# Projecting the values of the dilated heads transposed, one pair of heads at a time, and turning them on TensorE

## The chip, the cores and the metric

One core of one Trainium2 chip runs one launch of the kernel. The metric is the device time of that launch in microseconds (us), taken over several runs. A profiled execution gives the trace that the sections below read. Its engines are TensorE (PE; PEld is its weight load), VectorE (DVE), ScalarE (ACT), GpSimd (POOL) and SyncE (SP, which issues nearly all transfers; "SPq" is its queue).

## The reference, cut to what matters

One decoder layer on 512 tokens of width 1024, all in float32: a SwiGLU feed-forward, a mixer, a second SwiGLU feed-forward, each behind an RMS norm, and a final norm. The change lies in the mixer:

```
h = RMSNorm(x);  [q | k | v of 12 A heads | q | k | v of 8 B heads | gate_A | gate_B] = h @ W_in
y_A = window attention; heads 0-3 see single tokens, heads 4-7 every 4th, heads 8-11 every 16th token
      y_A of head h = merge of heads h, 4 + h, 8 + h
y_B = block attention of the 8 B heads
x = x + (sigmoid(gate_A) * (y_A @ W_up_A) + sigmoid(gate_B) * (y_B @ W_up_B)) @ W_out
```

A dilated head (4 to 11) attends within classes of tokens. The kernel works with four classes, tokens t with the same t mod 4, and needs the values of a dilated head as four tiles of 128 tokens of one class by 64 features.

## The kernel before, in words

**Numbers.** Every float32 operand of a matmul is split into a high and a low part (fp32r), and a product is three matmuls: high by high, high by low, low by high. `mac` (lines 203 to 208) issues the three. Activations are kept transposed, 8 tiles `XN[k]` of 128 features by 512 tokens, and a projection of 128 columns is 8 `mac` calls, 24 matmuls of 512 columns. The scale of the RMS norm is applied after the product: `factors` (L244) makes one row of it, `rrow`, for all tokens, and `columns` (L259) picks it as columns for token tiles.

**Weights.** One list, `stream`, holds the 512 KB weight tiles in order of use. `weights` (L193) returns the next, splits the one behind it (cast on ScalarE L189, subtraction on VectorE L190) and starts the transfer of the third behind it on the SP queue (L171).

**Mixer.** It begins inside the last tile of the first feed-forward: `FIRST` lists what is projected before the attention, `BESIDE` what is projected beside each of its 16 stages. Stages alternate: the scores of a head (`dsa_scores`, for head h the heads h, 4 + h and 8 + h), then its weighted sum. `blend` mixes the steps of a stage (main) and of its projections (side) evenly; a side step is one `mac`. The items are `qk n` (Q and K of the n-th pair of `PAIRS`: pair 0 is heads 0 and 1, pair 1 is heads 4 and 8, pair 2 is heads 5 and 9), `v c` (values of four undilated heads), `vd` (values of the dilated heads) and `g` (gates).

- `qk` : `project` and `stacked` (L459 to L485). The 128 by 512 sums of Q or K are scaled by `rrow` into a scratch tile `qkv` (L469, VectorE; dilated pairs are put in class order here), cast (L471, ScalarE), subtracted (L472, VectorE) into `qkhl` (2 buffers), and four transfers on the SP queue move the halves to Q (L483) or K (L485) tiles. The scratch tile has **one buffer, tag `ssq`**, which the row of the norm (`step`) uses before it.
- `vd` : `values_by_class` (L521). All eight heads at once. The 16 tiles of `XN` are copied on ScalarE with their tokens in class order (L534, `xc`, 3 buffers for each half). The copies are the stationary operands and 512 columns of weights move: 32 `mac` calls into **four** PSUM banks of the group `acc`, which has four and is also used by `qk`, `v` and `g`. `keep_values` then splits the sums (L517 ScalarE, L518 VectorE).

**Order.** TensorE runs in the order in which the program is written. The order on the other engines and on the SP queue is set when the kernel is built, by a planner that takes whatever is ready in its own model, earlier written first; on the chip each queue keeps that order.

```
FIRST = [("qk", 0), ("qk", 1), ("qk", 2), ("vd", 0)]
BESIDE = [ [("v", 0)], [("qk", 3)],  [("g", 0)], [("qk", 4), ("g", 1, 0)], ...
heads = [dsa(h) for h in range(4)] + [moba(h) for h in range(0, NB, 2)]
```

Of the kernel before, what the change touches and what calls it, by code (L numbers as in the profile page):

```python
# [23 lines left out]
F32 = mybir.dt.float32  # L24
# [4 lines left out]
P = 128  # L29
# [20 lines left out]
def slopes(n):  # L50
# [4 lines left out]
LAG = 2  # L55
WAIT = 5
LEAD = 9


FIRST = [("qk", 0), ("qk", 1), ("qk", 2), ("vd", 0)]  # L60
BESIDE = [
    [("v", 0)], [("qk", 3)],
    [("g", 0)], [("qk", 4), ("g", 1, 0)],
    [("qk", 5)], [("qk", 6)],
    [("g", 1, 1), ("v", 3)], [("qk", 7)],
    [("qk", 8)], [("v", 4)],
# [28 lines left out]
def decoder_layer(ctx: ExitStack, tc: tile.TileContext, xT, gains, gus, gu1, dn1, wqk, wv, wvd, wg, wup, wout, gu2, dn2, base, out):  # L95
# [35 lines left out]
    make_identity(nc, ident)  # L131


    cols_of = {}
    for name, shape in (("rcol0", [P, NT]), ("rcol1", [P, NT]), ("nv0", [P, 4, 2]), ("nv1", [P, 4, 2]), ("round", [P, 32])):
        cols_of[name] = cpool.tile(shape, F32, name=name)


    CHUNKS = [slice(c * P, min(c + 8, FT) * P) for c in range(0, FT, 8)]

    def mixer_tiles(what, n, *js):
        src = {"qk": lambda j: wqk[2 * n + j], "v": lambda j: wv[max(0, n - 2), j], "vd": lambda j: wvd[j], "g": lambda j: wg[2 * n + j]}[what]
        return [((what, n, j), src(j)) for j in js or range(4 if what == "vd" else 2)]

    def down_tiles(i, dn):
        return [((i, "d", m, c), dn[m][:, cut]) for m in range(KT) for c, cut in enumerate(CHUNKS)]
# [109 lines left out]
        newton(y, z, a, row)  # L256
        return row

    def columns(row, dilated):  # L259

        col = cols_of[f"rcol{int(dilated)}"]
        rest = tpool.tile([P, P], F32, name="rest", tag="fu")
        for t in range(NT):
            nc.vector.tensor_tensor_reduce(rest, tokens(row, t, dilated), ident, 1.0, 0.0, ALU.mult, ALU.max,
                                           accum_out=col[:, t:t + 1])
        return col

    def tokens(x, t, dilated):

        return by_class(x)[:, t] if dilated else x[:, t * P:(t + 1) * P]  # L270


    def first_tiles():
# [61 lines left out]
    def last_tile(A):  # L335

        m = KT - 1
        halves = [slice(h * HALF, (h + 1) * HALF) for h in range(2)]
        ps = [bank("all")[:, :HALF] for _ in range(2)]
        pc = [bank("all")[:, :2] for _ in range(2)]  # L340
        pr = [bank("all")[:, :HALF] for _ in range(2)]
        sq = [tpool.tile([P, HALF], F32, name=f"sql{h}", tag=("fg", "fu")[h]) for h in range(2)]
        v = [cols_of[f"nv{h}"] for h in range(2)]

        def some(h, k):
            mac(ps[h], cols(ws[k // 8], k % 8), [x[:, halves[h]] for x in A[k]], k == 0, k == FT - 1)

        def close(h):
            x = X[m][:, halves[h]]
            nc.vector.scalar_tensor_tensor(x, ps[h], 0.5, x, ALU.mult, ALU.add)  # L350
            nc.scalar.activation(sq[h], x, AF.Square)

        def sums(h, x, first):
            for t in range(2):
                nc.tensor.matmul(pc[h][:, t:t + 1], x[:, t * P:(t + 1) * P], ones[:, 0:1], start=first and t == 0,
                                 stop=not first and t == 1)

        def spread(h):
            a, y, z, col = (v[h][:, n] for n in range(4))
            nc.vector.tensor_scalar(a, pc[h], 1.0 / D, EPS, ALU.mult, ALU.add)  # L360
            newton(y, z, a, col)
            diag = tpool.tile([P, 2, P], F32, name="diag", tag=("fg", "fu")[h])
            for t in range(2):
                nc.vector.tensor_scalar(diag[:, t], ident, col[:, t:t + 1], None, ALU.mult)
            return diag

        def write(h, diag):
            nc.tensor.matmul(pr[h], ones, diag.rearrange("p t q -> p (t q)"), start=True, stop=True)
            row = tpool.tile([P, HALF], F32, name="rrow", tag=("rrow", "ssq")[h], bufs=1)
            nc.scalar.copy(row, pr[h])  # L370

            def scaled():
                for k in range(KT):
                    o = outs[h, k]
                    if k == m:
                        nc.vector.scalar_tensor_tensor(o, X[k][:, halves[h]], gain(k), pr[h], ALU.mult, ALU.mult)
                    elif k % 3 == 1 if h else k < 6:
                        nc.gpsimd.tensor_tensor(o, o, row, ALU.mult)
                    else:
                        nc.vector.tensor_tensor(o, o, pr[h], ALU.mult)  # L380
                    if k % 2:
                        nc.sync.dma_start(out[h, k // 2], pairs[h, k // 2].rearrange("p k t -> p (k t)"))
            return scaled

        def gain(k):
            return g_sb[:, 3 * KT + k:3 * KT + k + 1]

        pairs, outs = {}, {}
        for h in range(2):
            for k in range(KT):  # L390
                if k % 2 == 0:
                    pairs[h, k // 2] = xpool.tile([P, 2, HALF], F32, name=f"yo{h}_{k}", tag=f"xh{k + h}")
                outs[h, k] = pairs[h, k // 2][:, k % 2]
                if k != m:
                    nc.scalar.mul(outs[h, k], X[k][:, halves[h]], gain(k))
        ws = [weights(2, "d", m, 0)]
        for k in range(8):
            some(0, k)
            some(1, k)
        ws.append(weights(2, "d", m, 1))  # L400
        ws.append(weights(2, "d", m, 2))
        for k in range(8, FT):
            some(0, k)
        close(0)
        for h in range(2):
            sums(h, SSQ[3][:, halves[h]], True)
        for k in range(8, FT):
            some(1, k)
            if k == 11:
                sums(0, sq[0], False)  # L410
                diag = spread(0)
            if k == FT - 2:
                first = write(0, diag)
        close(1)
        sums(1, sq[1], False)
        diag = spread(1)
        first()
        warm_up(9)
        write(1, diag)()
# [18 lines left out]
    with ExitStack() as mix:  # L438
# [56 lines left out]
        def values(c):  # L495
# [11 lines left out]
                            k == 0 and t % 2 == 0, k == KT - 1 and t % 2 == 1)  # L507
                        yield
            for t in range(NT):
                keep_values(t, c, ps[t // 2][:, (t % 2) * n:(t % 2 + 1) * n], R["col"][False])  # L510

        def keep_values(t, c, pv, col):

            v = V[t, c] = mp.tile([P, 4 * P], F32R, name=f"v{t}_{c}", tag=f"v{t}_{c % 3}", bufs=1)
            heads = v.rearrange("p (h c) -> p h c", c=P)
            pv = pv.rearrange("p (h c) -> p h c", c=HD)
            nc.scalar.mul(heads[:, :, :HD], pv, col[:, t:t + 1])  # L517
            nc.vector.scalar_tensor_tensor(heads[:, :, HD:], pv, col[:, t:t + 1], f32(heads[:, :, :HD]),  # L518
                                           ALU.mult, ALU.subtract)

        def values_by_class():  # L521

            ps = [bank("acc") for _ in range(NT)]
            n = 8 * HD
            for quarter in range(4):
                w = weights("vd", 0, quarter)
                for kk in range(2):
                    k = 2 * quarter + kk  # L530
                    copies = []
                    for x, tag in zip(XN[k], ("pth", "ptl")):
                        xc = mp2.tile([P, S], F32R, name="xc", tag=tag, bufs=3)
                        nc.scalar.copy(xc.rearrange("p (r i) -> p r i", r=NT), by_class(x))  # L534
                        copies.append(xc)
                    for r in range(NT):
                        mac(ps[r], [x[:, r * P:(r + 1) * P] for x in copies], cols(w, kk, n), k == 0, k == KT - 1)
                        yield
            for r in range(NT):
                for c in (1, 2):  # L540
                    keep_values(r, c, ps[r][:, (c - 1) * 4 * HD:c * 4 * HD], R["col"][True])

        def bias(*parts):

# [93 lines left out]
        def weighted(steps, ytile, half, classes=False):  # L638
# [9 lines left out]
            for at in range(len(steps) + LAG):  # L648
# [20 lines left out]
                if at >= LAG:  # L669
                    for v, to, first, n in steps[at - LAG][1]:  # L670
                        for x in parts[at - LAG]:
                            done += 1
                            nc.tensor.matmul(to(po), V[v[0], v[1] // 4][:, v[1] % 4 * P:(v[1] % 4 + 1) * P], x[:, first:first + n],  # L673
                                             start=done == 1, stop=done == 2 * n_products)
                yield
            a, b = slice(half * HD, (half + 1) * HD), slice((1 - half) * HD, (2 - half) * HD)
# [68 lines left out]
        def part(what, n, *js):  # L745
# [3 lines left out]
            if what == "v":  # L749
                return values(n), NT * KT  # L750
            if what == "vd":
                return values_by_class(), NT * KT
            js = js or range(2)
            return (step for j in js for step in gate(n, j)), len(js) * KT


        early = []
# [2 lines left out]
                pass  # L760
            early.append(ps)
        R["row"] = factors(1, bank("out"))
        R["col"] = [columns(R["row"], dilated) for dilated in (False, True)]
        for j in range(2):
            stacked(0, j, early[j])
        for item in FIRST[1:]:
            for _ in part(*item)[0]:
                pass

        heads = [dsa(h) for h in range(4)] + [moba(h) for h in range(0, NB, 2)]  # L770
        for at, main in enumerate(x for h in heads for x in h):
            lead = LEAD * (2 if BESIDE[at][0][0] == "v" else 1)
            blend(main, [part(*item) for item in BESIDE[at]], lead if at % 2 else 0)


        YS = []
# [134 lines left out]
```

## Time and profile before

| | |
|---|---|
| median of 3 runs | 1140.09 us (1139.19 to 1141.45) |
| the profiled execution, its own time | 1141.3 us |
| its span, first to last instruction | 1139.4 us |
| mean granted clock of TensorE | 0.994 of full speed |
| busy share: PE, DVE, ACT, POOL | 98%, 52%, 38%, 2% |
| first matmul of the mixer, of the scores of head 0 | 365.8 us, 434.1 us |

A time in the text is that of the trace, in us from the start of the span. A row of a timeline gives start, duration, engine, line, operation, and in brackets how long the engine had been idle and what ended that. Matmuls overlap, so the distance between two starts is what a matmul costs, and not its duration.

### The profile page before, as it was taken

Reading aid. Unit: us, or ns where it says so; the run is one execution under the profiler, and the core shown is the slowest. Engines: PE = TensorE matmul, PEld = TensorE weight load, DVE = VectorE, ACT = ScalarE, POOL = GpSimd, SP = SyncE. Lnnn points to the kernel's source line nnn. Section 1 sums busy time; section 2 is a strip of 40 time slices with the busy share of each in tenths; the row PEclk is TensorE's granted clock in tenths of the full one; section 3 lists DMA queues with packets and bytes.
Section 4 is the critical chain, followed back from the end, with each engine's and each line's share of the span. In section 5 each row is a group of like instructions: output and inputs, shape, how many; then the busy total and the mean of one; then the engine's idle time right before and its main releaser. Section 6 shows DMA issues by size and latency. Waiting matters only on the chain.

```text
span 1139.4 us, 13537 instructions
## 1 busy us (share of the span) xinstructions
PE 1122.2 (98%) x5316; PEld 940.4 (83%) x5316; DVE 598.1 (52%) x976; ACT 429.1 (38%) x657; POOL 18.7 (2%) x34
## 2 busy tenths in 40 slices
PE   9999999999999989999999999999999999999997
PEld 7888888888888768888898888888888888888886
DVE  6744445433333637767777668654644445433323
ACT  5532233222223455444454454433333223223321
POOL 0000000000000000000000000000000000000001
PEclk9999999999999989999999999999999999999999
DMA  6222322233333382456354213332322232233321
GB/s 222 93 93 96 100 100 93 93 102 91 100 102 116 100 219 85 129 148 167 107 153 129 76 47 102 111 96 93 107 93 93 95 109 93 93 102 86 99 83 74
DMA packets 37710, 122.12 MB, mean 107 GB/s; under 512 B 4880, under 2 KB 4880, under 8 KB 37648
## 3 DMA queue, kind: packets, MB, share of 16 engines
q1 hardware_dynamic: 37072, 120.08, 34.1%
q10 hardware_dynamic: 576, 1.20, 0.3%
q8 instruction: 41, 0.67, 0.2%
q14 instruction: 21, 0.17, 0.0%
HBM read 103.44 MB, written 2.10 MB: 93 GB/s over the span
## 4 chain that ended last, share of the span: by engine, by line
PE 64%; DVE 2%; DMA 1%; ACT 1%; issue 0%; SPq 0%; DVEq 0%; ACTq 0%
PE ps_all L208 11%; PE ps_all L206 11%; PE ps_all L207 11%; PE ps_acc L206 8%; PE ps_acc L207 8%; PE ps_acc L208 8%; PE ps_out L673 2%; PE ps_att L654 1%; PE ps_att L207 1%; PE ps_att L208 1%; PE ps_att L206 1%; PE ps_att L629 1%; DMA ks<-qkhl 1%; PE ps_att L571 0%; DVE wlo L190 0%; PE ps_att L583 0%
## 5 line engine op out<-in xcount | busy, mean ns | idle before, releaser
L189 ACT CAST whi<-raw 128x1024 fp32r<-128x1024 f32 (+2 forms) x201 | 203.0, 1012 | 546.2 <-PE ps_all L207 254.9
L190 DVE TENSOR_TENSOR wlo<-raw,whi 128x1024 fp32r<-128x1024 f32 (+2 forms) x202 | 236.3, 1172 | 173.6 <-ACT whi L189 173.4
L206 PE MATMUL ps_all<-xh,whi 128*128 128x512 f32 x672 | 261.4, 389 | 0.0
L207 PE MATMUL ps_all<-xl,whi 128*128 128x512 f32 x672 | 261.4, 389 | 0.0
L208 PE MATMUL ps_all<-xh,wlo 128*128 128x512 f32 x672 | 261.4, 389 | 0.0
L207 PEld LDWEIGHTS ps_all<-xl,whi 128*128 128x128 f32 x672 | 126.1, 188 | 26.4
L208 PEld LDWEIGHTS ps_all<-xh,wlo 128*128 128x128 f32 x672 | 126.1, 188 | 26.1
L206 PEld LDWEIGHTS ps_all<-xh,whi 128*128 128x128 f32 x672 | 126.1, 188 | 26.1
L206 PE MATMUL ps_all<-ah,whi 128*128 128x512 f32 (+1 forms) x374 | 141.2, 377 | 0.0
L208 PE MATMUL ps_all<-ah,wlo 128*128 128x512 f32 (+1 forms) x374 | 140.8, 377 | 0.0
L207 PE MATMUL ps_all<-al,whi 128*128 128x512 f32 (+1 forms) x374 | 140.8, 376 | 0.0
L206 PE MATMUL ps_acc<-xh,whi 128*128 128x512 f32 x272 | 110.4, 406 | 0.0
L208 PE MATMUL ps_acc<-xh,wlo 128*128 128x512 f32 x272 | 106.4, 391 | 0.0
L207 PE MATMUL ps_acc<-xl,whi 128*128 128x512 f32 x272 | 106.3, 391 | 0.0
L297 DVE TENSOR_TENSOR fu<-ps_all,rrow 128x512 f32<-128x512 f32 x44 | 30.4, 691 | 124.1 <-PE ps_all L208 124.1
L206 PEld LDWEIGHTS ps_all<-ah,whi 128*128 128x128 f32 x374 | 70.4, 188 | 13.0
L207 PEld LDWEIGHTS ps_all<-al,whi 128*128 128x128 f32 x374 | 70.4, 188 | 13.0
L208 PEld LDWEIGHTS ps_all<-ah,wlo 128*128 128x128 f32 x374 | 70.4, 188 | 12.7
L295 DVE TENSOR_TENSOR fg<-ps_all,rrow 128x512 f32<-128x512 f32 x44 | 30.4, 691 | 79.8 <-PE ps_all L208 79.7
L208 PEld LDWEIGHTS ps_acc<-xh,wlo 128*128 128x128 f32 x272 | 51.1, 188 | 11.4
L207 PEld LDWEIGHTS ps_acc<-xl,whi 128*128 128x128 f32 x272 | 51.4, 189 | 7.2
L206 PEld LDWEIGHTS ps_acc<-xh,whi 128*128 128x128 f32 x272 | 51.2, 188 | 7.2
(168 smaller groups left out, 1256.3 us busy)
## 6 DMA issues: line engine op xcount, KB each, us to landing
raw<-in_gu_dram SPq DMA_DIRECT2D x84, 512.0 KB, 3.4
raw<-in_dn_dram SPq DMA_DIRECT2D x32, 512.0 KB, 3.5
raw<-in_wqk_dram SPq DMA_DIRECT2D x20, 512.0 KB, 3.5
ks<-qkhl SPq DMA_DIRECT2D x40, 256.0 KB, 4.9
raw<-in_wg_dram SPq DMA_DIRECT2D x16, 512.0 KB, 3.5
raw<-in_dn_dram SPq DMA_DIRECT2D x16, 384.0 KB, 3.1
qs<-qkhl SPq DMA_DIRECT2D x40, 128.0 KB, 2.5
raw<-in_wout_dram SPq DMA_DIRECT2D x8, 512.0 KB, 3.4
```

The costliest lines, as they stand in the source:

```text
L189: nc.scalar.copy(hi[:, s], raw[:, s])
L190: nc.vector.tensor_tensor(lo[:, s], raw[:, s], f32(hi[:, s]), ALU.subtract)
L206: nc.tensor.matmul(ps, wh, xh, start=first, stop=False)
L207: nc.tensor.matmul(ps, wh, xl, start=False, stop=False)
L208: nc.tensor.matmul(ps, wl, xh, start=False, stop=last)
L295: nc.vector.tensor_tensor(g, ps[0], R, ALU.mult)
L297: nc.vector.tensor_tensor(u, ps[1], R, ALU.mult)
L629: nc.tensor.matmul(ps[:, :n], Q[NA + h][:, i * P:(i + 1) * P], K[NA + h][:, part, :n], start=part == 0, stop=part == 1)
L654: nc.tensor.transpose(pt[:, n * P:(n + 1) * P], block, ident)
L673: nc.tensor.matmul(to(po), V[v[0], v[1] // 4][:, v[1] % 4 * P:(v[1] % 4 + 1) * P], x[:, first:first + n], start=done == 1, stop=done == 2 ...
```

## The change

The dilated values are projected the other way round: 128 columns of weights (one pair of heads) are stationary and the 512 tokens move, 24 matmuls into one PSUM bank, as for `qk`. VectorE scales the sums by `rrow` and puts the tokens in class order in one instruction, into the scratch tile with tag `ssq` (`vt`). Four TensorE transposes turn it into a bank of the group `att`, and a ScalarE copy and a VectorE subtraction split it. The transposes (`turned`) are issued behind the 6th step of whatever item follows. There are four such items, `vd 0` to `vd 3` (heads 4 and 5, 6 and 7, 8 and 9, 10 and 11). Two stand in `FIRST`, two move beside the scores and the weighted sum of head 1. `qk 1` becomes the last item of `FIRST`, and `qk 2` moves beside the scores of head 0. The copies `xc`, the second set of columns of the norm and the four wide banks go. The tiles of the values get other tags, and the host lays out the same weights differently.

```diff
-FIRST = [("qk", 0), ("qk", 1), ("qk", 2), ("vd", 0)]
+LATER = 5
+FIRST = [("qk", 0), ("vd", 0), ("vd", 2), ("qk", 1)]
 BESIDE = [
-    [("v", 0)], [("qk", 3)],
-    [("g", 0)], [("qk", 4), ("g", 1, 0)],
+    [("qk", 2), ("v", 0)], [("qk", 3)],
+    [("vd", 1), ("g", 0)], [("vd", 3), ("qk", 4), ("g", 1, 0)],
...
-    def columns(row, dilated):
+    def columns(row):
...
-            ps = [bank("acc") for _ in range(NT)]
-            n = 8 * HD
-            for quarter in range(4):
-                w = weights("vd", 0, quarter)
-                for kk in range(2):
-                    k = 2 * quarter + kk
-                    copies = []
-                    for x, tag in zip(XN[k], ("pth", "ptl")):
-                        xc = mp2.tile([P, S], F32R, name="xc", tag=tag, bufs=3)
-                        nc.scalar.copy(xc.rearrange("p (r i) -> p r i", r=NT), by_class(x))
-                        copies.append(xc)
-                    for r in range(NT):
-                        mac(ps[r], [x[:, r * P:(r + 1) * P] for x in copies], cols(w, kk, n), k == 0, k == KT - 1)
-                        yield
+        def values_by_class(n):
+            w = weights("vd", n, 0)
+            ps = bank("acc")
+            for k in range(KT):
+                mac(ps, cols(w, k), XN[k], k == 0, k == KT - 1)
+                yield
+            vt = tpool.tile([P, S], F32, name="qkv", tag="ssq", bufs=1)
+            nc.vector.tensor_tensor(vt.rearrange("p (r i) -> p r i", r=NT), by_class(ps), by_class(R["row"]), ALU.mult)
+            TURN.append((n, vt))
+
+        def turned():
+            n, vt = TURN.pop()
+            pt = bank("att")
             for r in range(NT):
-                for c in (1, 2):
-                    keep_values(r, c, ps[r][:, (c - 1) * 4 * HD:c * 4 * HD], R["col"][True])
+                nc.tensor.transpose(pt[:, r * P:(r + 1) * P], vt[:, r * P:(r + 1) * P], ident)
+            v = mp.tile([P, NT, 2, P], F32R, name=f"vd{n}", tag=f"vd{n}", bufs=1)
+            x = pt.rearrange("p (r h c) -> p r h c", r=NT, h=2)
+            nc.scalar.copy(v[:, :, :, :HD], x)
+            nc.vector.tensor_tensor(v[:, :, :, HD:], x, f32(v[:, :, :, :HD]), ALU.subtract)
...
+        def parts(items):
+            for item in items:
+                for at, _ in enumerate(part(*item)[0]):
+                    if at == LATER and TURN:
+                        turned()
+                    yield
+            if TURN:
+                turned()
...
-        R["col"] = [columns(R["row"], dilated) for dilated in (False, True)]
+        R["col"] = columns(R["row"])
         for j in range(2):
             stacked(0, j, early[j])
-        for item in FIRST[1:]:
-            for _ in part(*item)[0]:
-                pass
+        for _ in parts(FIRST[1:]):
+            pass
...
-            blend(main, [part(*item) for item in BESIDE[at]], lead if at % 2 else 0)
+            blend(main, [(parts(BESIDE[at]), sum(part(*item)[1] for item in BESIDE[at]))], lead if at % 2 else 0)
...
-        "wvd": _moving(v[:, 256:768], 2),
+        "wvd": _tiles(v[:, 256:768]),
```

## Rows read from the trace of the kernel before

**Rows 1.** What TensorE waited for: releaser, us in total, times, longest.

```profile
PE ps_acc L206 <- DVE qkv L469: 4.7, 2, 2.8
PE ps_att L206 <- ACT xh L222: 1.8, 1, 1.8
```

**Rows 2.** Timeline of TensorE, 365 to 382 us, the projection of pair 0.

```profile
365.83 0.39 PE L206 MATMUL ps_att<-xh,whi 128*128 128x512 f32 x1
...
370.37 0.39 PE L208 MATMUL ps_att<-xh,wlo 128*128 128x512 f32 x1
372.57 0.50 PE L206 MATMUL ps_att<-xh,whi 128*128 128x512 f32 x1 [1.82 <-ACT xh L222]
...
381.27 0.39 PE L250 MATMUL ps_out<-sl,ones_r 128*128 128x512 f32 x1
381.50 0.39 PE L206 MATMUL ps_acc<-xh,whi 128*128 128x512 f32 x1
```

**Rows 3.** Timeline of ScalarE, 366 to 373 us.

```profile
366.77 1.13 ACT L534 CAST xc<-xh 128x512 fp32r<-128x512 f32 x1
...
371.80 0.72 ACT L222 ACTIVATE xh<-x,g_sb 128x512 fp32r<-128x512 f32 x1
```

**Rows 4.** Timeline of VectorE, the end of the first feed-forward.

```profile
366.03 0.69 DVE L330 SCALAR_TENSOR_TENSOR x<-ps_all,x 128x512 f32<-128x512 f32 x1 [1.99 <-PE ps_all L208]
```

**Rows 5.** Timeline of TensorE, 403 to 433 us, all of `vd`.

```profile
403.26 0.39 PE L206 MATMUL ps_acc<-whi,xc 128*128 128x512 f32 x1
...
404.39 0.39 PE L208 MATMUL ps_acc<-whi,xc 128*128 128x512 f32 x1
...
407.57 0.47 PE L206 MATMUL ps_acc<-whi,xc 128*128 128x512 f32 x1 [2.79 <-DVE qkv L469]
...
410.39 0.76 PE L206 MATMUL ps_acc<-whi,xc 128*128 128x512 f32 x1 [1.89 <-DVE qkv L469]
...
432.90 0.36 PE L206 MATMUL ps_acc<-whi,xh 128*128 128x256 f32 x1 [0.21 <-DVE v L518]
```

**Rows 6.** Stretches: length, busy us of each engine, PEclk, DMA share, GB/s.

```profile
375.00:377.00 2.00, 2.00 (x6) 1.52 (x5) 1.83 (x2) 0.54 (x2) 0.00 (x0) 0.50 0.02 4
...
411.00:415.00 4.00, 4.00 (x11) 3.13 (x10) 0.69 (x1) 1.81 (x3) 0.00 (x0) 0.50 0.86 204
...
450.00:460.00 10.00, 10.00 (x56) 8.43 (x56) 8.41 (x22) 4.92 (x8) 0.00 (x0) 1.00 0.54 150
```

**Rows 7.** Timeline of TensorE, four transposes in a weighted sum.

```profile
453.90 0.60 PE L654 MATMUL ps_att<-ident,prow 128*128 128x128 f32 x4
454.25 0.48 PE L206 MATMUL ps_acc<-xh,whi 128*128 128x512 f32 x1
454.57 0.40 PE L207 MATMUL ps_acc<-xl,whi 128*128 128x512 f32 x1
```

**Rows 8.** Timeline of VectorE, 390 to 398 us, from `rrow` on.

```profile
390.28 0.68 DVE L241 SCALAR_TENSOR_TENSOR rrow<-step,root 128x512 f32<-128x512 f32 x1
...
391.63 0.69 DVE L469 SCALAR_TENSOR_TENSOR qkv<-ps_att,rrow 128x512 f32<-128x512 f32 x1
...
393.49 0.69 DVE L472 TENSOR_TENSOR qkhl<-qkv,qkhl 128x512 fp32r<-128x512 f32 x1
...
394.38 0.70 DVE L469 SCALAR_TENSOR_TENSOR qkv<-ps_att,rrow 128x512 f32<-128x512 f32 x1
...
396.12 0.70 DVE L472 TENSOR_TENSOR qkhl<-qkv,qkhl 128x512 fp32r<-128x512 f32 x1
396.85 1.05 DVE L469 SCALAR_TENSOR_TENSOR qkv<-ps_acc,rrow 128x512 f32<-128x512 f32 x1
```

**Rows 9.** Timeline of ScalarE, 392 to 414 us: a cast of Q that waits.

```profile
413.19 0.62 ACT L471 CAST qkhl<-qkv 128x512 fp32r<-128x512 f32 x1 [5.07 <-DMA ks<-qkhl]
```

**Rows 10.** Timeline of the SP queue, the transfers of K of pair 1.

```profile
406.37 3.00 SPq L485 DMA_DIRECT2D ks<-qkhl  x4
```

**Rows 11.** Tile `ks`: from the issue of a transfer of K to its landing.

```profile
DMA to landing us min/median/max: 2.9/4.9/6.1
```

More of the change, by code (lines that the diff above doesn't have):

```diff
@@ L131, in decoder_layer @@
     make_identity(nc, ident)
-    cols_of = {}
-    for name, shape in (("rcol0", [P, NT]), ("rcol1", [P, NT]), ("nv0", [P, 4, 2]), ("nv1", [P, 4, 2]), ("round", [P, 32])):
-        cols_of[name] = cpool.tile(shape, F32, name=name)
+    rcol = cpool.tile([P, 2 * NT], F32, name="rcol")
+    nvs = [cpool.tile([P, 4, 2], F32, name=f"nv{h}") for h in range(2)]
+    cpool.tile([P, 40], F32, name="round")
     CHUNKS = [slice(c * P, min(c + 8, FT) * P) for c in range(0, FT, 8)]
     def mixer_tiles(what, n, *js):
-        src = {"qk": lambda j: wqk[2 * n + j], "v": lambda j: wv[max(0, n - 2), j], "vd": lambda j: wvd[j], "g": lambda j: wg[2 * n + j]}[what]
-        return [((what, n, j), src(j)) for j in js or range(4 if what == "vd" else 2)]
+        src = {"qk": lambda j: wqk[2 * n + j], "v": lambda j: wv[max(0, n - 2), j], "vd": lambda j: wvd[n], "g": lambda j: wg[2 * n + j]}[what]
+        return [((what, n, j), src(j)) for j in js or range(1 if what == "vd" else 2)]
     def down_tiles(i, dn):
@@ L257, in factors @@
         return row
-    def columns(row, dilated):
-        col = cols_of[f"rcol{int(dilated)}"]
+    def columns(row):
         rest = tpool.tile([P, P], F32, name="rest", tag="fu")
         for t in range(NT):
[L264 to L270, printed above, removed]
+            nc.vector.tensor_tensor_reduce(rest, row[:, t * P:(t + 1) * P], ident, 1.0, 0.0, ALU.mult, ALU.max,
+                                           accum_out=rcol[:, t:t + 1])
+        return rcol
     def first_tiles():
@@ L342, in last_tile @@
         sq = [tpool.tile([P, HALF], F32, name=f"sql{h}", tag=("fg", "fu")[h]) for h in range(2)]
-        v = [cols_of[f"nv{h}"] for h in range(2)]
+        v = nvs
         def some(h, k):
@@ L509, in values @@
             for t in range(NT):
[L510 to L519, printed above, removed]
@@ L521, in values_by_class @@
-        def values_by_class():
-            ps = [bank("acc") for _ in range(NT)]
-            n = 8 * HD
-            for quarter in range(4):
-                w = weights("vd", 0, quarter)
-                for kk in range(2):
-                    k = 2 * quarter + kk
-                    copies = []
-                    for x, tag in zip(XN[k], ("pth", "ptl")):
-                        xc = mp2.tile([P, S], F32R, name="xc", tag=tag, bufs=3)
-                        nc.scalar.copy(xc.rearrange("p (r i) -> p r i", r=NT), by_class(x))
-                        copies.append(xc)
-                    for r in range(NT):
-                        mac(ps[r], [x[:, r * P:(r + 1) * P] for x in copies], cols(w, kk, n), k == 0, k == KT - 1)
-                        yield
-            for r in range(NT):
-                for c in (1, 2):
-                    keep_values(r, c, ps[r][:, (c - 1) * 4 * HD:c * 4 * HD], R["col"][True])
+                if c == 4:
+                    if t % 2 == 0:
+                        pair = mp.tile([P, 2, 4 * P], F32R, name=f"v{t}_{c}", tag=f"vd{t // 2}", bufs=1)
+                    v = pair[:, t % 2]
+                else:
+                    v = mp.tile([P, 4 * P], F32R, name=f"v{t}_{c}", tag=f"v{t}", bufs=1)
@@ new lines, in values @@
+                heads = v.rearrange("p (h c) -> p h c", c=P)
+                pv = ps[t // 2][:, (t % 2) * n:(t % 2 + 1) * n].rearrange("p (h c) -> p h c", c=HD)
+                nc.scalar.mul(heads[:, :, :HD], pv, R["col"][:, t:t + 1])
+                nc.vector.scalar_tensor_tensor(heads[:, :, HD:], pv, R["col"][:, t:t + 1], f32(heads[:, :, :HD]),
+                                               ALU.mult, ALU.subtract)
+                for h in range(4):
+                    V[t, 4 * c + h] = heads[:, h]
@@ new lines, in values_by_class @@
+        def values_by_class(n):
[7 more added lines that the diff above has]
+            TURN.append((n, vt))
+        TURN = []
+        def turned():
+            n, vt = TURN.pop()
+            pt = bank("att")
+            for r in range(NT):
+                nc.tensor.transpose(pt[:, r * P:(r + 1) * P], vt[:, r * P:(r + 1) * P], ident)
[3 more added lines that the diff above has]
+            nc.vector.tensor_tensor(v[:, :, :, HD:], x, f32(v[:, :, :, :HD]), ALU.subtract)
+            for h in range(2):
+                for r in range(NT):
+                    V[r, 4 + 2 * n + h] = v[:, r, h]
@@ L672, in weighted @@
                             done += 1
-                            nc.tensor.matmul(to(po), V[v[0], v[1] // 4][:, v[1] % 4 * P:(v[1] % 4 + 1) * P], x[:, first:first + n],
+                            nc.tensor.matmul(to(po), V[v], x[:, first:first + n],
                                              start=done == 1, stop=done == 2 * n_products)
@@ L751, in part @@
             if what == "vd":
-                return values_by_class(), NT * KT
+                return values_by_class(n), KT
             js = js or range(2)
             return (step for j in js for step in gate(n, j)), len(js) * KT
+        def parts(items):
[6 more added lines that the diff above has]
+                turned()
         early = []
```

## The prediction

> **What bounds the kernel now.** I read the busy shares first. TensorE is busy for nearly the whole span, so only three things can change the time: what TensorE is given, how long it stands, and its clock. The list of what TensorE waited for is short, and its two largest entries lie where the change works [rows 1]. So I read TensorE's timeline there and count against its undisturbed pitch. From 381.50 [rows 2] to 403.26 [rows 5] stand 96 matmuls of 512 columns, 0.2267 us each.
>
> First stretch: from 365.83 to 381.50 stand 50 such matmuls, worth 11.34 us, and they took 15.67, so 4.33 are lost [rows 2]. The bracket names ScalarE's `xh`, the cast of the last tile of x. Its input was there at 366.72 (366.03 + 0.69) [rows 4], but ScalarE ran five copies `xc` for the dilated values first, from 366.77 to 371.90, and the cast began only at 371.80 [rows 3].
>
> Second stretch: from 403.26 to 432.90 stand the 96 matmuls of `vd`, worth 21.76 us. They took 29.64, so 7.88 are lost [rows 5]. `vd` needs four banks of `acc` at once. The third and fourth still hold `qk 2`, which VectorE can't read out because the single scratch tile is held by a cast that waits for K's transfers (such a wait of 5.07 stands in the queue of casts [rows 9]).
>
> Of both losses a part is clock and restart: 4.33 less a wait of 1.8, and 7.88 less 4.7 [rows 1], leave 2.5 and 3.2. Behind each wait the granted clock stands at 0.50 (1.2 GHz) while TensorE is fully busy, for at least 2 and 4 us [rows 6], which costs half of that, 1.0 and 2.0.
>
> **What it removes.** The copies `xc` go, so the cast of the last tile can start at about 366.9. TensorE needs it at 370.6. The first loss goes whole, 4.33. Each new item of `vd` takes one bank, and only four are taken up to the end of `FIRST`, so the second loss goes too, 7.88. Together -12.2 us. Everything behind pair 0 moves up by 4.33.
>
> **Equal or hidden.** The matmuls of `vd` stay 96 of 512 columns, and the weights stay four tiles of 512 KB. `vd 1` and `vd 3` move 48 matmuls (10.9 us of TensorE) behind the scores' start. That is the same sum elsewhere. Their `turned` comes six side steps (4.1 us) after the last product, main steps in between, and `vt` needs one VectorE instruction of 1.05. If that cover is gone, it costs about 1 each. I take 0 and keep 2 for the upper end. ScalarE loses 16 copies (1.1 each) and gains four; VectorE loses four short reductions. Neither engine is the bound. `qk 2` moves beside the scores of head 0, and its eight transfers, two stages ahead of their use, cost nothing there.
>
> **Transposes.** 16 are added, in four groups. Four of them in a weighted sum took 0.35 from start to start, and the next matmul 0.09 over its pitch [rows 7]. So 4 x 0.44 = 1.8 us. The Trainium skill, TensorE: Matmul & The Clock Gate, Part 4, speaks against the change here: it gives about 275 ns for a transpose in a kernel and says that the full clock does not engage in that mode. Laid end to end at 275 ns (an estimate from that page), 16 would cost 4.4 and the sum below would be 2.6 higher. The trace differs: a start every 0.09 [rows 7], at a granted clock of 1.00 in the stretch that holds them [rows 6].
>
> **New wait 1, the first `turned`.** TensorE starts `vd 0` at 381.50 - 4.33 = 377.17. Eight steps and then six of `vd 2` are 42 matmuls, 9.52 us, so it asks for `vt` at 386.69. `vt` needs `rrow`, which ended at 390.96 [rows 8], now at 386.63. It also needs the scratch tile, and two `qkv` tiles of pair 0 are written earlier in the program. Before, the third user of that tile was a dilated `qkv`, which began at 396.85 [rows 8], 5.9 behind `rrow`. With four reductions and a weight split out of the way I add bare durations: 0.67 until the first `qkv`, then 0.69 + 0.62 + 0.69 and 0.70 + 0.62 + 0.70 for the two tiles (write, cast, subtract; the casts from [rows 9]), 0.16 of hand-overs, 1.05 for `vt` in class order. That is 5.9, so 392.5. TensorE stands 5.8. Lower end: `vt` takes the tile first, 388.35, a wait of 1.7. Upper end: the old start less the shift, 393.57, a wait of 6.9. Queued behind it are two steps of `vd 2` and all of `qk 1`, so nothing makes it up.
>
> **New wait 2, the first scores.** They read Q and K of pair 1, and `qk 1` is now the last item of `FIRST`. 48 side steps stand to 13 main steps, so only four steps of `qk 2`, 2.7 us, lie between the end E of `qk 1` and the first scores. Before, all of `qk 2` and `vd` lay there. K's last sums are there at E + 0.16. Then come 1.05 (dilated scaling), 0.62, 0.70 and hand-overs, and the first transfer is issued at E + 2.7. Four issues take 3.00 [rows 10], so the last starts 2.25 later. Landing takes 2.9, 4.9 or 6.1 (least, middle, most) [rows 11]. That gives E + 7.9, 9.9 or 11.1. Issue to release before, 406.37 [rows 10] to 413.19 [rows 9], was 6.8 and gives E + 9.5. TensorE asks at E + 2.7. I take a wait of 7.0, between 5.1 and 8.4. Behind it on TensorE stand the rest of `qk 2` and `v 0`, which need nothing from it but can't pass.
>
> **Clock.** Each of the two waits is longer than the ones after which the clock stood at 0.50. I take 2.2 for each, between 1.0 and 3.2 (above).
>
> **Sum.** -12.2 + 1.8 + 5.8 + 2.2 + 7.0 + 2.2 = +6.8 us. The profiled execution took 1141.3, so 1148.1 for such a one. It stood 1.2 above the median of the runs, so against the median 1147 us, slower by 0.6%. Behind 434 us no wait of TensorE is listed but a few of a microsecond at the very end, so nothing later takes it up. The low ends of all terms give -12.2 + 1.8 + 2.7 + 6.1 = -1.6, or 1138.5; the high ends give -12.2 + 1.8 + 10.1 + 11.6 + 2 = +13.3, or 1153.4.
>
> **Rivals.**
> *The scratch tile goes to `vt` first* (not slower). One mechanism, in VectorE's queue behind `rrow`: if the planner puts `vt` ahead of the two `qkv` tiles, wait 1 is 1.7 with no clock behind it. The sum is -12.2 + 1.8 + 1.7 + 9.2 = +0.5, or 1140.6. It decides from the point where `vt` ends before about 389. For it: TensorE stands for `vt` and for no `qkv`. Against it: the rows show the tile handed on in written order [rows 8]. 13%.
> *One of the two waits hardly exists* (faster). K lands before TensorE asks, or `vt` is early and K's transfers land at their fastest. -12.2 + 1.8 + 8.0 = -2.4, or 1137.7; with both short, 1138.5 or, without the clock's price, 1136.5. Against it: 1.05 + 0.62 + 0.70 of arithmetic alone fill the 2.7 us that four steps cover, before any transfer starts. 17%.
> *K's transfers are queued behind weight tiles on the SP queue* (slower still). A 512 KB tile put ahead of them lengthens wait 2 by 2 to 5 us: 1149 to 1152. For it: a transfer of K took up to 6.1 to land where others ran. 12%.
>
> **How the numbers follow.** 58% for the forecast. A measurement of this kernel can tell 0.2%, 2.3 us, from no change. Slower than 1142.4: the forecast but for its low tail, and the third rival, 67%. Faster than 1137.8: 17%. Between: the first rival and the tail, 16%. The range of the forecast alone is 1142 to 1152. The range 1137 to 1152 takes in the first rival and half of the second, and leaves out the rest of that and the upper tail.
>
> **What would show it.** In the trace of the changed kernel: no `xc`, and 365.8 to 377.2 for pair 0 without a gap; a wait of TensorE's transposes on VectorE's `qkv` of about 6 us near 387; a wait of the first scores (L571's successor) of about 7 us near 411, whose release is the transfer of K; granted clock 0.50 behind both; no wait in the stages that hold `vd 1` and `vd 3`. I am wrong if `vt` is written before pair 0's second `qkv`, or if the first scores start within 3 us of the fourth step of `qk 2`.

## The result and the profile after

The changed kernel takes 1153.08 us (median, 1152.94 to 1153.41) against 1140.11 before: ratio 1.0113, 95% interval 1.0096 to 1.0131. It is slower by 13.0 us. The forecast said slower, 1147 us, and its range ended at 1152.

The list of what TensorE waited for, after (releaser, us in total, times, longest); it answers to [rows 1].

```profile
PE ps_att L578 <- DMA ks<-qkhl: 9.1, 3, 6.1
PE ps_att L541 <- DVE qkv L531: 5.6, 1, 5.6
```

Both old entries are gone. In their place stand one wait of the transposes (L541) on `vt` (L531 on VectorE) and **three** waits of the first scores of a head (L578) on transfers of K. I had named two places; the third is new. TensorE's timeline shows all three, with what stands behind each.

```profile
387.15 0.39 PE L210 MATMUL ps_acc<-xh,wlo 128*128 128x512 f32 x1
393.17 1.09 PE L541 MATMUL ps_att<-ident,qkv 128*128 128x128 f32 x4 [5.64 <-DVE qkv L531]
393.91 0.78 PE L208 MATMUL ps_acc<-xh,whi 128*128 128x512 f32 x1
...
400.83 0.60 PE L541 MATMUL ps_att<-ident,qkv 128*128 128x128 f32 x4
401.19 0.48 PE L208 MATMUL ps_acc<-xh,whi 128*128 128x512 f32 x1
401.50 0.39 PE L209 MATMUL ps_acc<-xl,whi 128*128 128x512 f32 x1
...
410.60 0.39 PE L210 MATMUL ps_acc<-xh,wlo 128*128 128x512 f32 x1
417.09 0.55 PE L578 MATMUL ps_att<-ks,qs 128*128 128x256 f32 x1 [6.11 <-DMA ks<-qkhl]
419.12 0.55 PE L578 MATMUL ps_att<-ks,qs 128*128 128x256 f32 x1 [1.48 <-DMA ks<-qkhl]
419.48 0.63 PE L208 MATMUL ps_acc<-xh,whi 128*128 128x512 f32 x1
419.91 0.63 PE L209 MATMUL ps_acc<-xl,whi 128*128 128x512 f32 x1
...
506.28 0.40 PE L210 MATMUL ps_acc<-xh,wlo 128*128 128x512 f32 x1
507.00 0.36 PE L578 MATMUL ps_att<-ks,qs 128*128 128x256 f32 x1 [0.33 <-PE ps_acc L210]
508.89 0.36 PE L578 MATMUL ps_att<-ks,qs 128*128 128x256 f32 x1 [1.54 <-DMA ks<-qkhl]
509.09 0.40 PE L208 MATMUL ps_acc<-xh,whi 128*128 128x512 f32 x1
...
514.99 0.45 PE L208 MATMUL ps_acc<-xh,whi 128*128 128x512 f32 x1
```

The distance from one start to the next, less the pitch, is what each cost. Wait 1 is 393.17 - 387.15 - 0.23 = 5.8. Wait 2 has two parts, because the scores read K of two heads and their transfers land apart: 417.09 - 410.60 - 0.23 = 6.3 and 419.12 - 417.09 less about 0.1 = 1.9. The third, at the scores of head 2, has two parts as well, 0.5 + 1.8 (for the first the profile names no transfer). Four transposes with cover take 0.36, and the next matmul 0.08 over its pitch, as in [rows 7].

The transfers of K behind wait 2 were issued at 411.15 on the SP queue:

```profile
411.15 3.17 SPq L482 DMA_DIRECT2D ks<-qkhl  x4
```

Behind each wait the starts are 0.43 apart and no longer 0.23. The stretches of the same trace give the clock (columns as in [rows 6]).

```profile
411.00:417.00 6.00, 0.00 (x0) 0.00 (x0) 0.12 (x1) 0.34 (x1) 0.00 (x0) 0.74 0.91 243
...
419.00:423.00 4.00, 3.88 (x10) 3.13 (x11) 0.86 (x3) 0.60 (x2) 0.00 (x0) 0.50 0.00 0
...
509.00:513.00 4.00, 4.00 (x14) 3.32 (x15) 2.23 (x8) 1.20 (x4) 0.00 (x0) 0.57 0.07 25
...
393.00:396.00 3.00, 2.83 (x9) 2.47 (x10) 0.72 (x2) 0.59 (x1) 0.00 (x0) 0.50 0.95 209
```

Full work at 0.50 (1.2 GHz) against 1.00 costs, counted in matmuls over their pitch, 1.7 behind wait 1 and 2.3 behind wait 2. Wait 3 is read against the same rows of the kernel before, because that kernel already lost a little there: its first two scores of head 2 take 0.59 up to the next matmul, and the next two 0.23.

```profile
497.99 0.39 PE L208 MATMUL ps_acc<-xh,wlo 128*128 128x512 f32 x1
498.21 0.74 PE L571 MATMUL ps_att<-ks,qs 128*128 128x256 f32 x2
498.80 0.39 PE L206 MATMUL ps_acc<-xh,whi 128*128 128x512 f32 x1
...
503.12 0.45 PE L206 MATMUL ps_acc<-xh,whi 128*128 128x512 f32 x1
```

From 506.28 to 509.09 it is 2.81 where it was 0.81 (497.99 to 498.80), so 2.0 of wait are new. From 509.09 to 514.99, the place of 503.12 in the changed kernel, it is 5.90 where it was 4.32, so the clock costs 1.6 there.

**The sum again, with measured terms:** -12.2 + 1.8 (transposes) + 5.8 + 1.7 + 8.2 + 2.3 + 2.0 + 1.6 = +11.2 us. Both traces can be measured over the same work, from the first matmul of the mixer to the first matmuls that end the scores of head 2. Changed kernel first, then the kernel before, whose first matmul stands in [rows 2]:

```profile
366.52 0.39 PE L208 MATMUL ps_att<-xh,whi 128*128 128x512 f32 x1
...
521.93 0.53 PE L604 MATMUL ps_att<-send,consts 128*128 128x32 f32 x4
```

```profile
510.06 0.53 PE L597 MATMUL ps_att<-send,consts 128*128 128x32 f32 x4
```

That is 155.41 against 144.23, 11.2 more, so the terms account for the mixer. The spans of the two profiled executions differ by 1151.1 - 1139.4 = 11.7. The rest, 0.7, stands ahead of the mixer, where nothing was changed (366.52 against 365.83), and behind these points the traces run level within 0.2. It is no effect of the change: in the runs below the mixer begins between 365.7 and 366.4, with the old projection and with the new. The medians differ by 13.0, because the profiled execution of the old kernel stood 1.2 above its median and that of the new one at its own.

### The profile page after: what moved, and what is told of

It reads as the page before. It is cut to its first block, busy times and chain, and to the rows that moved or that the text cites. A ratio compares the mean times of both kernels' runs of the same rounds, so it can differ in the third digit from the quotient of the medians.

```text
span 1151.1 us, 13539 instructions
## 1 busy us (share of the span) xinstructions
PE 1126.2 (98%) x5332; PEld 944.4 (82%) x5332; DVE 600.7 (52%) x968; ACT 413.1 (36%) x637; POOL 20.0 (2%) x34
## 4 chain that ended last, share of the span: by engine, by line
PE 95%; DVE 2%; DMA 2%; issue 0%; SPq 0%; ACT 0%; DVEq 0%; ACTq 0%
PE ps_all L208 20%; PE ps_all L210 20%; PE ps_all L209 20%; PE ps_acc L208 8%; PE ps_acc L210 8%; PE ps_acc L209 8%; PE ps_all L280 2%; PE ps_out L680 2%; PE ps_att L208 1%; PE ps_att L210 1%; PE ps_att L661 1%; PE ps_att L209 1%; DMA ks<-qkhl 1%; PE ps_att L636 1%; DMA raw<-in_wqk_dram 0%
## 5 line engine op out<-in xcount | busy, mean ns | idle before, releaser
L208 PE MATMUL ps_acc<-xh,whi 128*128 128x512 f32 x304 | 125.3, 412 | 0.0
L209 PE MATMUL ps_acc<-xl,whi 128*128 128x512 f32 x304 | 120.7, 397 | 0.0
L210 PE MATMUL ps_acc<-xh,wlo 128*128 128x512 f32 x304 | 120.6, 397 | 0.0
L210 PEld LDWEIGHTS ps_acc<-xh,wlo 128*128 128x128 f32 x304 | 58.2, 191 | 13.1
L209 PEld LDWEIGHTS ps_acc<-xl,whi 128*128 128x128 f32 x304 | 58.7, 193 | 8.5
L208 PEld LDWEIGHTS ps_acc<-xh,whi 128*128 128x128 f32 x304 | 58.5, 193 | 8.6
```

The costliest lines, as they stand in the source:

```text
L208: nc.tensor.matmul(ps, wh, xh, start=first, stop=False)
L209: nc.tensor.matmul(ps, wh, xl, start=False, stop=False)
L210: nc.tensor.matmul(ps, wl, xh, start=False, stop=last)
```

## Experiments

The first three change one thing each and keep the new projection.

**`qk 2` back into `FIRST`, behind `qk 1`.**

```diff
-FIRST = [("qk", 0), ("vd", 0), ("vd", 2), ("qk", 1)]
+FIRST = [("qk", 0), ("vd", 0), ("vd", 2), ("qk", 1), ("qk", 2)]
-    [("qk", 2), ("v", 0)], [("qk", 3)],
+    [("v", 0)], [("qk", 3)],
```

> The changed kernel with qk 2 back in FIRST, behind qk 1. Theory: the wait of the first scores (8.2 us in two parts, released by the transfers of K) comes from the place of qk 1 as the last item, and the clock behind it costs 2.3 more. With 10.9 us of qk 2 between, K lands in time: that wait is gone and the time falls by 10.5, from 1153.1 to about 1142.6. Rival: K's transfers are slow whatever lies between, because the SP queue is blocked in the new order; then the wait only moves and the time falls by less than 4, to 1149 or more. Both expect the first wait for vt (5.8) and the one at the scores of head 2 to stay.

Measured 1141.85 us, 11.2 below the changed kernel, ratio to the old one 1.0016 (1.0007 to 1.0025). TensorE's waits:

```profile
PE ps_att L541 <- DVE qkv L531: 5.7, 1, 5.7
PE ps_att L578 <- DMA ks<-qkhl: 1.7, 1, 1.7
```

Wait 2 is gone in both parts and the other two stand within 0.2 of what they were. The place of `qk 1` cost 8.2 + 2.3 = 10.5 by the trace and 11.2 by the times. K's transfers are not slow in themselves.

**`vd 3` behind `qk 4`, beside the weighted sum of head 1.**

```diff
-    [("vd", 1), ("g", 0)], [("vd", 3), ("qk", 4), ("g", 1, 0)],
+    [("vd", 1), ("g", 0)], [("qk", 4), ("vd", 3), ("g", 1, 0)],
```

> The changed kernel with vd 3 behind qk 4 beside the weighted sum of head 1, nothing else. Theory: the third wait (scores of head 2, near 507 us, on the transfer of K of qk 4) is there because vd 3 pushes qk 4 towards its reader; with vd 3 behind it the wait (2.2) and its slow clock (1.9) go: 1153.1 - 4.1 = 1149.0. Rival: the wait comes from more transfers and VectorE work in that stage and not from the order: it stays and the time is within 1 us of 1153.1.

Measured 1149.55 (1149.12 to 1149.81), 3.5 below, against 2.0 + 1.6 by the trace; the 4.1 of the expectation still held the old kernel's own loss at that place. The third wait is gone, with the same instructions in the stage:

```profile
PE ps_att L578 <- DMA ks<-qkhl: 7.6, 2, 6.2
```

So it was the order. The old trace already said how little room there was. The SP queue issued K of `qk 4` here in the kernel before:

```profile
491.41 3.76 SPq L485 DMA_DIRECT2D ks<-qkhl  x4
```

The first scores of head 2 start at 498.21 there (the rows above). That is 6.8 us from issue to use, and the same 6.8 that I had read for a set of K's transfers [rows 9, 10]. TensorE lost under 0.4, and there was nothing to spare. After the change the issue stands here:

```profile
500.94 3.39 SPq L482 DMA_DIRECT2D ks<-qkhl  x4
```

TensorE asks at 506.5, 5.6 later, and goes on at 508.9. `vd 3` ahead of `qk 4` puts the end of `qk 4` at side step 24 of 32 (before: 16 of 24). Eight side steps remain in both, but the main steps are spread over more side steps, and of the twelve only five are left instead of eight. So the scores come 9.2 us behind the end of `qk 4` (497.33 to 506.5) instead of 10.5 (487.71 to 498.21), while the issue follows that end by 3.6 and 3.7.

**A buffer of its own for `vt`.**

```diff
-            vt = tpool.tile([P, S], F32, name="qkv", tag="ssq", bufs=1)
+            vt = tpool.tile([P, S], F32, name="vt", tag="vt", bufs=1)
```

> The changed kernel with a buffer of its own for vt, instead of the scratch tile of Q and K. Theory: the first wait (5.8) is the queue for that tile behind the two tiles of pair 0; with its own buffer vt can be written while ScalarE casts the first, near 388.5 to 389.6 in the changed kernel's trace, against TensorE's request at 387.4, so the wait is 2 to 2.5 us and 3.5 us are won, 4 with the clock: 1149 to 1149.6. Rival: vt waits for rrow and VectorE's own work and not for the tile: the wait stays over 5 and the time within 1 us of 1153.1.

Measured 1147.42 (1147.20 to 1147.71), 5.7 below, more than expected. VectorE's timeline, first of the changed kernel and then of this one:

```profile
387.69 0.68 DVE L466 SCALAR_TENSOR_TENSOR qkv<-ps_att,rrow 128x512 f32<-128x512 f32 x1
...
389.88 0.69 DVE L466 SCALAR_TENSOR_TENSOR qkv<-ps_att,rrow 128x512 f32<-128x512 f32 x1
...
391.25 0.69 DVE L469 TENSOR_TENSOR qkhl<-qkv,qkhl 128x512 fp32r<-128x512 f32 x1 [0.68 <-ACT qkhl L468]
391.98 1.05 DVE L531 TENSOR_TENSOR qkv<-ps_acc,rrow 128x512 f32<-128x512 f32 x1
```

```profile
386.98 0.69 DVE L466 SCALAR_TENSOR_TENSOR qkv<-ps_att,rrow 128x512 f32<-128x512 f32 x1
387.58 1.06 DVE L531 TENSOR_TENSOR vt<-ps_acc,rrow 128x512 f32<-128x512 f32 x1
```

In the first, `vt` is the third user of the tile and starts 0.04 behind the subtraction that frees it. In the second it starts right behind the first `qkv`. TensorE's wait falls from 5.6 to 2.0, and in this execution the clock stays at 1.00 behind it, so the 1.7 goes as well: 3.6 + 1.7 = 5.3 of the 5.7.

```profile
389.00:394.00 5.00, 5.00 (x25) 4.18 (x24) 4.81 (x10) 2.17 (x3) 0.00 (x0) 1.00 0.51 118
```

The 2.0 that remain are not the tile: `vt` then waits for `rrow` and the first `qkv` on VectorE.

**All three together.** The edits above in one kernel.

> The changed kernel with all three: qk 2 back in FIRST, vd 3 behind qk 4, vt in its own buffer. Theory: the three waits are separate and lie one behind the other on TensorE, so what they gave alone adds up: 11.2 + 3.5 + 5.7 = 20.4 below 1153.1, that is 1132.7, faster than the old kernel by 7.5. What is left above the sum of the removed losses is the wait for vt of 2.0. Rival: the waits are linked (K of pair 1 starts earlier when the first wait is shorter, so the second was partly counted twice, or a new one opens at another reader of K): 1136 or more.

Measured 1134.51 (1133.07 to 1134.72), ratio to the old kernel 0.9946 (0.9929 to 0.9962): 18.6 below the changed kernel, where the single gains add up to 20.4. The only wait left in the mixer is the 2.0 for `vt`. The time lies about halfway between the two theories' numbers. Most of the missing 1.8 stands in the trace, and needs no link between the waits: behind this wait, as long as with the own buffer alone, TensorE's clock fell.

```profile
389.36 0.66 PE L541 MATMUL ps_att<-ident,vt 128*128 128x128 f32 x4 [1.96 <-DVE vt L531]
```

```profile
390.00:393.00 3.00, 3.00 (x9) 2.32 (x8) 2.03 (x8) 1.97 (x3) 0.00 (x0) 0.50 0.75 175
```

That costs 1.6 here and cost nothing in that run. The other executions have no trace; the fastest of the four, 1133.07, had a mean granted clock of 0.999 and the others 0.996 to 0.997.

**The same, with `qk 1` directly behind pair 0.**

```diff
-FIRST = [("qk", 0), ("vd", 0), ("vd", 2), ("qk", 1)]
+FIRST = [("qk", 0), ("qk", 1), ("vd", 0), ("vd", 2), ("qk", 2)]
```

> As all three, but with qk 1 directly behind pair 0 in FIRST: qk 0, qk 1, vd 0, vd 2, qk 2. Theory: vd 0 then ends 10.9 us later, long behind rrow, so the last 2.0 of the first wait go too, and K of pair 1 lands while vd 0, vd 2 and qk 2 run: 1130 to 1131. Rival: qk 1 right behind pair 0 finds both qkhl buffers held by pair 0's transfers, its K is late and VectorE and the banks back up, so a wait opens at qk 2 or at the first scores: 1134 or more.

Measured 1130.28 (1129.97 to 1130.77), ratio to the old kernel 0.9913 (0.9898 to 0.9928). TensorE has no wait at all in the mixer. 1140.1 less the removed 12.2 and with 1.8 for transposes is 1129.7, which is this within 0.6.

**The same order, `vt` in the shared scratch tile again.** The kernel just above without the buffer of its own.

> The reordered kernel (qk 0, qk 1, vd 0, vd 2, qk 2 in FIRST, vd 3 behind qk 4) with vt in the scratch tile of Q and K again. Theory: the tile then is held by qk 1's second half until pair 0's transfers free a qkhl buffer, so the turning of vd 0 waits 2 to 5 us with the clock behind it, and the order alone is not enough: 1133 to 1137. Rival: with vd 0 so late the tile is free and its own buffer gave nothing: 1130 to 1131.

Measured 1137.55 (1136.68 to 1138.50), 7.3 above, a little more than the theory's range. The cast of `qk 1`'s second half, from ScalarE's timeline, and `vt`, from VectorE's, both of this kernel:

```profile
400.73 0.62 ACT L468 CAST qkhl<-qkv 128x512 fp32r<-128x512 f32 x1 [5.70 <-DMA ks<-qkhl]
```

```profile
402.10 1.05 DVE L531 TENSOR_TENSOR qkv<-ps_acc,rrow 128x512 f32<-128x512 f32 x1
```

The tile is held by a cast that waits for pair 0's transfers; TensorE's transposes wait 5.1 for it, and the slow clock behind costs 2.6. In the new projection, order and buffer are both needed.

**Wait 2 filled with work.** 36 matmuls that nobody reads stand ahead of the first scores of head 0; they are added work and change no output.

```diff
+            if h == 0:
+                spare = bank("out")
+                for _ in range(36):
+                    nc.tensor.matmul(spare, XN[0][0][:, :P], XN[0][0], start=True, stop=True)
```

> The changed kernel with 36 matmuls of 512 columns added ahead of the first scores of head 0; they read the first activation tile, write a bank that nobody reads, and last 8.2 us, as long as the second wait in its two parts. Theory: the 0.43 us pitch behind the wait (419.5 to 423.8) is the granted clock of 0.50 and comes from the idle time alone. With TensorE busy through the wait the clock stays at 1.00, the wait is filled at no cost and 2.2 to 2.4 us are won: 1150.8. Rival: the slow stretch is not the clock of an idle engine but what the scores themselves wait for, and the added work is paid: 1153 to 1161.

Measured 1149.03 (1148.48 to 1151.48), 4.1 below. TensorE's timeline and the clock of the stretch:

```profile
411.29 8.32 PE L577 MATMUL ps_out<-xh 128*128 128x512 f32 x36
419.45 0.64 PE L582 MATMUL ps_att<-ks,qs 128*128 128x256 f32 x2
419.94 0.40 PE L208 MATMUL ps_acc<-xh,whi 128*128 128x512 f32 x1
420.17 0.40 PE L209 MATMUL ps_acc<-xl,whi 128*128 128x512 f32 x1
```

```profile
411.00:417.00 6.00, 6.00 (x29) 4.95 (x28) 0.59 (x1) 0.81 (x1) 0.00 (x0) 1.00 0.88 235
```

From the end of the fourth side step to the next one behind the scores it is 8.9 us with the added matmuls and 8.9 without, and behind it the pitch is 0.23 where it was 0.43. 8.2 us of added work are free and bring back the clock's 2.3 at this place. The profiled execution is only 1.6 below the changed kernel's, because the slow clock behind wait 1 cost it 2.6 and not 1.7, with the wait itself unchanged (5.7):

```profile
393.00:398.00 5.00, 5.00 (x15) 4.03 (x15) 2.16 (x3) 1.63 (x2) 0.00 (x0) 0.50 0.84 196
```

That the median fell by 4.1 and not 2.3 stays open: the profiled execution is the slowest of the four (1151.48), and the others have no trace.

**The old kernel, one loss at a time.** First the copies `xc` held behind the cast of the last tile of x.

```diff
+                        with tc.issue_after(state["xh"]):
+                            nc.scalar.copy(xc.rearrange("p (r i) -> p r i", r=NT), by_class(x))
```

> The kernel before, with the class-ordered copies held behind ScalarE's cast of the last tile of x, nothing else. Theory: the first loss of the old kernel (4.33 us near 371) is five copies that ScalarE ran ahead of that cast. Held behind it they cost TensorE nothing there, and the copies of the first tiles are still in time for vd at 403: 1140.1 - 4.3 = 1135.8. Rival: the cast was late for another reason (its input, VectorE), or the copies are late where they are then needed: 1138 or more.

Measured 1137.21 (1136.37 to 1138.54), ratio 0.9973 (0.9964 to 0.9982): 3.0 faster by the medians. The wait on `xh` is gone; the one for the banks of `acc` stays:

```profile
PE ps_acc L206 <- DVE qkv L469: 4.2, 2, 3.0
```

Pair 0's 48 matmuls take 10.88 in this trace (365.94 to 376.82), 48 times the pitch, so the 4.33 are gone from that place. The profiled executions differ by 1141.3 - 1136.9 = 4.4. The medians give less, and the rival's 1138 lies inside the spread of the runs. The cause is shown; what it is worth over several executions is nearer 3 than 4.4, and why is open.

Then the sums of `vd` in other banks.

```diff
-            ps = [bank("acc") for _ in range(NT)]
+            ps = [bank("att") for _ in range(3)] + [bank("out")]
```

> The kernel before, with the four sums of vd in the three banks of att and the one of out instead of the four of acc, nothing else. Theory: the second loss of the old kernel (7.88 us from 403 to 433) is the third and fourth bank of acc still held by qk 2, with the clock behind it. In the other banks vd starts at once; the first scores then wait for a bank of att that the values' split still reads, 0.4 to 1.5 us. 1140.2 - 7.9 + 1 = 1133.3. Rival: the copies in class order or the weights are late as well, and the loss only changes its name: 1137 or more.

Measured 1137.69 (1136.48 to 1139.27), ratio 0.9979 (0.9970 to 0.9988): 2.5 faster where I expected 6.9. The wait for banks is gone, but others stand in its place, these two the largest:

```profile
PE ps_att L206 <- ACT whi L189: 1.7, 1, 1.7
...
PE ps_att L207 <- DVE wlo L190: 0.8, 1, 0.8
```

ScalarE's timeline says why:

```profile
413.59 0.62 ACT L471 CAST qkhl<-qkv 128x512 fp32r<-128x512 f32 x1 [3.17 <-DMA ks<-qkhl]
414.12 1.11 ACT L534 CAST xc<-xh 128x512 fp32r<-128x512 f32 x1
415.12 1.05 ACT L189 CAST whi<-raw 128x1024 fp32r<-128x1024 f32 x1
```

A cast of Q or K waits for transfers, and the cast of the weights that TensorE needs is queued behind it and a copy `xc`. The banks were only the nearest of two effects of three `qk` in a row; the rival was right.

**The old projection without its waits.** Copies held as above, the other banks, and `vd` between `qk 1` and `qk 2`.

```diff
-FIRST = [("qk", 0), ("qk", 1), ("qk", 2), ("vd", 0)]
+FIRST = [("qk", 0), ("qk", 1), ("vd", 0), ("qk", 2)]
```

> The kernel before with its own projection of the values, but its waits taken away by order alone: the copies held behind the cast of the last tile of x, vd between qk 1 and qk 2, and its sums in the banks of att and out. Theory: what the old kernel loses is order, not the way in which the values are projected. Without the 12.2 us of losses, and with up to 1.5 us for the second bank of att that pair 0 still holds, it takes 1128 to 1130.5, level with or below the reordered new projection (1130.3), which pays 1.8 us for its transposes. Rival: ScalarE, with ten copies of 1.1 us beside the casts of weights within 22 us of vd, falls behind as it did with other banks alone, and it takes 1133 or more.

Measured 1130.37 (1129.87 to 1131.50), ratio 0.9914 (0.9899 to 0.9929), level with 1130.28 of the reordered new projection. One wait is left in the mixer:

```profile
PE ps_att L206 <- DVE qkv L469: 1.2, 1, 1.2
```

So between these two kernels the way of projecting the values is worth nothing, in either direction. The old one pays with this wait and with 16 copies on ScalarE that fit beside the matmuls once they are in the right place, the new one with 1.8 us of transposes. What moves the time is where things stand: the order of `qk` and `vd` and the place of the copies, with the banks (old) or the buffer (new) that the order needs. The run changes three of these at once and does not say what each is worth in the old kernel.

## Why the prediction was wrong

- **The losses of the old kernel**, 4.33 and 7.88: right. Both stretches are gone in the changed kernel, and with all waits removed the time is within 0.6 us of the sum. My account of the second was too short: not the banks alone, also ScalarE's queue.
- **Transposes**, 1.8: right, 0.36 + 0.08 for four with cover. The 275 ns that the Trainium skill, TensorE: Matmul & The Clock Gate, Part 4, gives for one in a kernel are not what one costs here: a start every 0.09, though one lasts 0.27 in the trace of the kernel before.
- **Wait 1**, 5.8: right in size (5.8), place and releaser; its clock was 1.7 where I took 2.2. That the tile is the cause of 3.6 of the idle 5.6 is shown by the own buffer; the other 2.0 are `rrow` and VectorE.
- **Wait 2**, 7.0 with 2.2 for the clock: mis-sized. It was 8.2 with 2.3. K's first transfer was issued at 411.15 and TensorE went on at 419.12, 8.0 later, where I took the 6.8 of one set. It lay inside my bounds.
- **The step that failed is "Equal or hidden"**: `vd 1` and `vd 3` "move 48 matmuls ... That is the same sum elsewhere". I checked the cover of their `turned` (no wait there, as predicted) and not what they push. `vd 3` pushes `qk 4` against its reader, and K of `qk 4` had no room left. That is the third wait, put at nothing and in truth 2.0 + 1.6 by the trace and 3.5 by the run that takes it away. The sign that I had named for it, no wait in the stages of `vd 1` and `vd 3`, held: the wait opened one stage later.
- **The median**: I took 1.2 off because the profiled execution of the old kernel was that much above its median. The changed kernel's executions lie within 0.5 us, so this belongs to the old kernel's spread and not to a forecast of the new one.

Without the third wait, with the other terms as measured and with the 1.2 left on, the forecast stands at 1149 and the range holds; the run without that wait measured 1149.55. The high ends of all terms, 1153.4, do reach the measured time, but with sizes that did not occur. The rivals: the scratch tile going to `vt` first did not happen (`vt` was its third user); no wait was missing; and no weight tile stood among K's four transfers in the SP queue, though one was issued just ahead of them, at 410.55.

## What to carry to other kernels

When a change moves a piece of work, list what it pushes as well as what it needs: for every producer that is followed by a transfer, measure in the old trace the time from issue to first use, and treat a distance that only just suffices as a wait to come. A tile with one buffer that several chains share makes the last chain wait for all, so look at the tags of scratch tiles before the engines' loads. And when a new form of a computation comes together with a new order, time the old form in the new order too: here that one run came out level with the best new one, and so took the whole gain away from the new form.

## What the runs showed that I had not expected

- The clock's price does not grow with the wait, and the wait does not fix it. Behind 5.8, 8.2 and 2.3 us of waiting it was 1.7, 2.3 and 1.6 us in the changed kernel. Behind the same 5.8 it was 1.4 with `qk 2` back in `FIRST`, 2.1 with `vd 3` behind `qk 4` and 2.6 with wait 2 filled. Behind 2.0 it was nothing with the own buffer and 1.6 with all three edits; behind 1.2 (old projection reordered) nothing. So one trace does not give this price to better than about 1 us.
- Matmuls that nobody reads, put into a wait, cost nothing there and kept the granted clock behind it at 1.00.
- K of two heads, issued in one set of four transfers, released TensorE at two times 2.0 us apart (417.09 and 419.12).
